# Gate and up of a SwiGLU block by seven products of halves instead of eight, with weight sums made once and fp32 transposes

## The chip, the cores and the metric

One core of one Trainium2 chip runs the whole kernel in one launch. The metric is the device time of one execution in microseconds, as the median of 3 runs. TensorE (PE) multiplies, VectorE (DVE), ScalarE (ACT) and GpSimd (POOL) do elementwise work, and SyncE (SP) issues nearly all DMAs, in order, to one queue that is served by 16 DMA engines.

## The reference

One layer of a hybrid encoder over 2048 tokens of width 1024, in float32. What the change touches is its last part:

```python
h = h + rms_norm(mix, ln_mix_post)          # mix = concat of 4 mixers @ w_out
a = rms_norm(h, ln_ffn_pre)
ff = (jax.nn.silu(a @ w_ffn_gate) * (a @ w_ffn_up)) @ w_ffn_down   # D_FF = 2816
h = h + rms_norm(ff, ln_ffn_post)
```

Ahead of it stand `a @ w_in` (1024 to 3084 columns) and four causal mixers (S5, HGRN2, FoX attention, mLSTM).

## The kernel before, in words

**Number format.** Every large product is made in three matmuls: an operand x is split in hi (x rounded to fp32r, by ACT) and lo (x - hi), and hi*hi + lo*hi + hi*lo are summed in PSUM. So each 128x128 weight tile is met by three matmuls per 512 tokens.

**Stages.** Tokens come in 4 blocks of 512, in two halves of two blocks. `in_proj` (its matmuls are L279 and L297) runs over 11 chunks of columns of `w_in` for the first half, then again for the second half. At chosen chunks it calls hooks: the mixers of block 0, their set-up, and in the second half `first`, which does `pre(0)` and `proj(0)` of the block 0. Work of mixers gets a high priority, and the framework's scheduler lays the instructions of all stages into one fixed order per engine. After `in_proj`, blocks 0 to 3 are gone through: `proj(b)` (matmuls L1394), the mixers of block b+1, then the feed-forward `run(b)` (gate and up L1477, down L1502). Mixer matmuls of block b+1 are so laid between the feed-forward matmuls of block b; block 3 has none beside it.

**Transposes.** Tokens lie on partitions and must be turned to put the contraction there. `transpose_parts` (L97 to L114) splits a tile of 128 tokens in hi and lo first (L104 ACT, L105 DVE or POOL), transposes both with fp32r matmuls against an identity (L109, 16 for a tile) and copies both out of PSUM (L112 ACT, L114 DVE). It is used for 16 tiles each in `in_proj`, `pre` and `proj`.

**proj.** `proj(b)` multiplies the mixers' outputs by `w_out` in two halves of 512 columns: the first for all 4 token tiles, the second tile by tile. After a tile's second half come a chain of small steps: scale and sum of squares, the residual `b_xt` by DMA (L1427; the pool `x` has 2 buffers), DVE L1428, ACT square L1340, POOL L69 and L70, DVE L1433, then the transposes.

**Feed-forward.** For each of 22 tiles f of 128 columns, gate and up take 24 matmuls of 512 tokens each. The first two f are cut in two halves of 256 tokens, so that the first half can run before the last two token tiles are transposed. `down` takes two f at a time, 48 matmuls of 512 columns. In block 0 each weight is loaded raw into a ring of 2 tiles `wr`, split (L89 ACT, L90 POOL), and both parts are also stored to DRAM; blocks 1 to 3 load the two parts, 1 MB for each gate or up tile, into a ring of 4 `wh` and 4 `wl`.

## Time and profile before

| | |
|---|---|
| median of 3 runs | 2833.97 us (2827.44 to 2839.25) |
| the profiled execution | 2835.35 us, span 2833.6 us, mean granted clock 0.984 |
| PE busy | 2720.2 us, 96% of the span |
| PE weight loads busy | 2294.8 us, 81% |
| DVE, POOL, ACT busy | 56%, 31%, 29% |
| DMA | 605 MB, mean 214 GB/s |
| matmuls of gate and up | 4608, 30% of the chain that ended last |
| matmuls of down | 2112, 15% of that chain |

Busy time of PE counts pipelined matmuls with modelled ends, so how fast they follow each other is read from distances of their starts. A stage's share of the DMA engines tells how much room a further transfer has there.

### The profile page before, as it was taken

To read this page: it belongs to the slowest core of one execution; us is meant where nothing else is said; L and a number is where in the kernel's file an instruction comes from. 1 tells how busy PE (TensorE), PEld (TensorE's weight loads), DVE (VectorE), ACT (ScalarE), POOL (GpSimd) and SP (SyncE) were. 2 spreads that over 40 slices of the span, in tenths; PEclk is the share of its full clock that TensorE was granted. 3 is DMA by queue.
4 is the path that set the end of the run, shared out by engine and by line. 5 is a ranking of instruction groups with operands and counts; after the bars stand their busy time and mean duration, and the time that the engine had idled before them with its cause. 6 is when DMAs were issued, how large, how long until landed. Compare 5 with 4: busy or idle time off the path is not lost.

```text
span 2833.6 us, 40116 instructions
## 1 busy us (share of the span) xinstructions
PE 2720.2 (96%) x14678; PEld 2294.8 (81%) x14678; DVE 1598.5 (56%) x2587; ACT 830.7 (29%) x1596; POOL 883.9 (31%) x959
## 2 busy tenths in 40 slices
PE   6898999999999999999999999999999999999998
PEld 5797987989888788788787777888877788888886
DVE  7968456575315666875566656645665654422323
ACT  6323326333324233324221222224122332300001
POOL 7554311253215466743211235222022432100001
PEclk9999999999999999999999999999999999999999
DMA  6673595554769887686846566475655656765553
GB/s 201 207 255 135 179 289 171 169 176 154 254 191 313 279 270 252 242 295 230 288 164 210 192 207 212 153 264 210 214 184 188 196 170 230 273 211 193 190 192 139
DMA packets 323108, 605.11 MB, mean 214 GB/s; under 512 B 56160, under 2 KB 146144, under 8 KB 322656
## 3 DMA queue, kind: packets, MB, share of 16 engines
...
q0 software_dynamic: 1024, 0.07, 0.0%
...
## 4 chain that ended last, share of the span: by engine, by line
PE 72%; DVE 11%; DMA 9%; issue 3%; POOL 2%; SPq 2%; ACT 2%; DVEq 0%; POOLq 0%; ACTq 0%
PE pf L1477 30%; PE pf L1502 15%; PE pf L297 6%; PE pf L279 5%; PE pf L1394 3%; PE ps L912 2%; DMA g_h<-h_d 1%; DVE hQ L520 1%; DMA b_xt<-in_x_dram 1%; PE ps L896 1%; PE ps L895 1%; PE ps L837 1%; DVE hA L534 1%; PE pt L109 1%; DVE xl L105 1%
## 5 line engine op out<-in xcount | busy, mean ns | idle before, releaser
L1477 PE MATMUL pf<-b_ah,wl 128*128 128x512 f32 (+1 forms) x1536 | 580.0, 378 | 0.0
L1477 PE MATMUL pf<-b_ah,wh 128*128 128x512 f32 (+1 forms) x1536 | 579.6, 378 | 0.3 <-DMA wh<-wg2h 0.3
L1477 PE MATMUL pf<-b_al,wh 128*128 128x512 f32 (+1 forms) x1536 | 579.7, 379 | 0.0
L1502 PE MATMUL pf<-dh,g_h 128*128 128x512 f32 x1408 | 458.8, 395 | 1.9 <-DVE b_acc L1507 1.8
L1477 PEld LDWEIGHTS pf<-b_ah,wh 128*128 128x128 f32 x1536 | 290.4, 189 | 55.0 <-issue 0.4
L1477 PEld LDWEIGHTS pf<-b_ah,wl 128*128 128x128 f32 x1536 | 290.5, 189 | 54.8
L1477 PEld LDWEIGHTS pf<-b_al,wh 128*128 128x128 f32 x1536 | 289.6, 189 | 54.3
L1502 PEld LDWEIGHTS pf<-dh,g_h 128*128 128x128 f32 x1408 | 263.3, 188 | 57.5 <-DVE b_acc L1507 2.9
L1502 PE MATMUL pf<-dl,g_h 128*128 128x512 f32 x704 | 276.5, 393 | 0.0
L1507 DVE TENSOR_TENSOR b_acc<-b_acc,pf 128x512 f32<-128x512 f32 x320 | 215.6, 683 | 102.1 <-PE pf L1502 100.2
L909 POOL TENSOR_TENSOR f_accs<-f_accs,f_pe 128x512 f32<-128x512 f32 (+3 forms) x144 | 172.4, 1197 | 285.0 <-ACT f_pe L903 281.8
L90 POOL TENSOR_TENSOR wl<-wr,wh 128x1024 fp32r<-128x1024 f32 (+2 forms) x76 | 187.5, 2471 | 223.6 <-ACT wh L89 194.9
L905 DVE TENSOR_TENSOR f_pl<-f_pe,f_ph 128x512 fp32r<-128x512 f32 (+3 forms) x160 | 187.0, 1176 | 94.5 <-ACT f_ph L904 78.2
L297 PE MATMUL pf<-wh,aTh 128*128 128x256 f32 (+2 forms) x768 | 219.8, 287 | 2.6 <-ACT stg L323 1.6
L297 PE MATMUL pf<-wl,aTh 128*128 128x256 f32 (+2 forms) x768 | 221.4, 288 | 0.0
L297 PE MATMUL pf<-wh,aTl 128*128 128x256 f32 (+2 forms) x768 | 220.3, 287 | 0.0
L1482 DVE SCALAR_TENSOR_TENSOR g_th<-g_th,pf 128x512 f32<-128x512 f32 x88 | 60.3, 685 | 198.7 <-ACT g_th L1481 198.1
L1481 ACT ACTIVATE g_th<-pf 128x512 f32<-128x512 f32 x88 | 52.7, 599 | 399.1 <-PE pf L1477 399.0
L279 PE MATMUL pf<-aTh,wh 128*128 128x512 f32 (+1 forms) x400 | 159.8, 400 | 1.0 <-ACT hnz L304 1.0
L279 PE MATMUL pf<-aTl,wh 128*128 128x512 f32 (+1 forms) x400 | 158.3, 398 | 2.5 <-DVE aTl L114 2.5
L903 ACT ACTIVATE f_pe<-ps 128x512 f32<-128x512 f32 (+3 forms) x160 | 85.4, 534 | 252.7 <-PE ps L896 106.7
L279 PE MATMUL pf<-aTh,wl 128*128 128x512 f32 (+1 forms) x400 | 159.1, 398 | 0.0
...
## 6 DMA issues: line engine op xcount, KB each, us to landing
...
```

The lines of the kernel that those rows point to most:

```text
L90: nc.gpsimd.tensor_tensor(lo, r, f32(hi), ALU.subtract)
L279: nc.tensor.matmul(l3(pt)[:, cut], lhsT=x[k][:, s], rhs=a[:, cut, k], start=(n == 0), stop=(n == 23))
L297: nc.tensor.matmul(pt[:, :w], lhsT=a[:, t, k], rhs=x[k], start=(n == 0), stop=(n == 23))
L903: nc.scalar.activation(pe[:, cs], pt[:, cs], AF.Exp)
L905: nc.vector.tensor_tensor(pl[:, cs], pe[:, cs], f32(ph[:, cs]), ALU.subtract)
L909: nc.gpsimd.tensor_tensor(accs[:, cs], accs[:, cs], pe[:, cs], ALU.add)
L912: nc.tensor.matmul(o, lhsT=w, rhs=r[:, cs], start=(kt + n == 0), stop=(kt + n == NK))
L1394: nc.tensor.matmul(pt, lhsT=a[:, t, k], rhs=w, start=(first and i == 0), stop=(last and i == 2))
L1477: nc.tensor.matmul(l3(pt)[:, s], lhsT=x[:, k], rhs=a[:, s, k], start=(k == 0 and i == 0), stop=(k == KD - 1 and i == 2))
L1482: nc.vector.scalar_tensor_tensor(th, th, 1.0, pts[0], ALU.add, ALU.mult)
L1502: nc.tensor.matmul(pt, lhsT=a[:, s], rhs=w[:, 0], start=(m == 0), stop=(m == 3 * len(fs) - 1))
L1507: nc.vector.tensor_tensor(acc[:, t, ns], acc[:, t, ns], pt, ALU.add)
```

## The change

**Seven products.** For a pair q of f tiles, the weights form a 2x2 of blocks (two f tiles by two halves of the 1024 contraction rows), and the tokens another (halves of the rows by even and odd token tiles). Instead of 8 block products the Strassen-Winograd scheme makes 7, from 3 plain blocks and 4 sums on the weight side and 3 plain blocks and 4 sums on the token side. `product(i)` does gate and up in one PSUM tile: 2 x 4 x 3 = 24 matmuls of 256 columns. The outputs are added up from PSUM by DVE (7 adds and one ACT copy for a pair q) before the gating.

**Weight sums.** `FfnWeights.make` runs 22 times, from hooks of `in_proj` (8 in the first half, 14 in the second): it loads two raw tiles, makes 4 sums on POOL (128x512 each) and stores 7 blocks to DRAM. The same hooks copy `w_ffn_down` and `w_out` to DRAM scratch `wd_d` and `wo_d` (30 copies of 512 KB). In the feed-forward, `load(q, i)` takes the raw product weights into the `wl` tile itself and splits them there by ACT and POOL; only for i = 0, 2 and 5 are the parts kept in DRAM, so blocks 1 to 3 split 4 of 7 products again. The ring `wr` is gone there.

**Token operands.** `proj` no longer transposes each tile: for each pair of token tiles, `operands` makes four differences (DVE and POOL) and transposes 7 blocks of 512 rows. All products read a tile `U` of 14 slots, which also holds the transposed mixer outputs before.

**Transposes** take the fp32 tile itself (L111 in the new file: 8 for a tile), and the split comes at the copy out of PSUM.

**Order.** `proj(0)` moves out of `in_proj` to the front of block 0. Mixers that run beside the feed-forward get fewer buffers (for example hQ 2 for 4, f_KB 2 for 3).

```diff
-def split_load(c, pool, raw, tag, width, shape, src, key=None, part=None):
+def split_load(c, pool, tag, width, n, src, key=None, raw=None):
...
+    x = f32(lo) if raw is None else raw.tile([P, WRING], F32, name="wr")[:, 0:n]
+    src(x)
+    nc.scalar.activation(hi, x, AF.Copy)
+    nc.gpsimd.tensor_tensor(lo, x, f32(hi), ALU.subtract)
...
-    for h in range(0, KD, 4):
-        hs = slice(h * P, (h + 4) * P)
-        hi, lo = (c.phl.tile([P, 512], F32R, name=n, tag="hl") for n in ("xh", "xl"))
-        nc.scalar.activation(hi, x[:, hs], AF.Copy)
-        eng.tensor_tensor(lo, x[:, hs], f32(hi), ALU.subtract)
-        for src, dst in ((hi, dh), (lo, dl)):
-            pt = pool.tile([P, 512], F32R, name="pt", tag=tag)
-            for j in range(4):
-                nc.tensor.transpose(pt[:, j * P:(j + 1) * P], src[:, j * P:(j + 1) * P], c.identr)
-            pv = pt.rearrange("p (k t) -> p k t", k=4)
-            if src is hi:
-                nc.scalar.activation(dst[:, h:h + 4], pv, AF.Copy)
-            else:
-                nc.vector.tensor_copy(dst[:, h:h + 4], pv)
+    for h in range(0, x.shape[1] // P, 4):
+        pt = pool.tile([P, 512], F32, name="pt", tag=tag)
+        for j in range(4):
+            nc.tensor.transpose(pt[:, j * P:(j + 1) * P], x[:, (h + j) * P:(h + j + 1) * P], c.ident)
+        pv = pt.rearrange("p (k t) -> p k t", k=4)
+        nc.scalar.activation(dh[:, h:h + 4], pv, AF.Copy)
+        nc.vector.tensor_tensor(dl[:, h:h + 4], pv, f32(dh[:, h:h + 4]), ALU.subtract)
...
-        nk = 4
+        nk, nq = (4, 4) if c.side == "right" else (3, 2)
...
-        hQ = [p1.tile([P, 2, 256], F32, name=f"hQ{p}") for p in range(nk)]
+        hQ = [p1.tile([P, 2, 256], F32, name=f"hQ{p}") for p in range(nq)]
...
+    def make(self, pool, q, m):
+        nc = self.c.nc
+        r1, r2 = (pool.tile([P, D], F32, name=n, tag=n) for n in ("ws_1", "ws_2"))
+        for r, f in ((r1, 2 * q), (r2, 2 * q + 1)):
+            nc.sync.dma_start(r.rearrange("p (k n) -> p k n", k=KD), self.w[m][:, :, f * P:(f + 1) * P])
+        a, b = slice(0, 512), slice(512, D)
+        X11, X12, X21, X22 = r1[:, a], r1[:, b], r2[:, a], r2[:, b]
+        for i, s in ((0, X11), (2, X12), (5, X22)):
+            nc.sync.dma_start(self.raw[q][i][:, m * 512:m * 512 + 512], s)
+        for i, s, x, y, op in ((3, X11, X11, X21, ALU.subtract), (4, X21, X21, X22, ALU.add),
+                               (1, X22, X22, X11, ALU.subtract), (6, X12, X12, X22, ALU.subtract)):
+            nc.gpsimd.tensor_tensor(s, x, y, op)
+            nc.sync.dma_start(self.raw[q][i][:, m * 512:m * 512 + 512], s)
+
+    def load(self, q, i):
+
+        c = self.c
+        return split_load(c, c.pw, "w", WRING, D, lambda t: c.nc.sync.dma_start(t, self.raw[q][i]),
+                          f"w{q}_{i}" if i in (0, 2, 5) else None)
...
+    def y(self, t):
+
+        i = 2 * (2 * (t % 2)) + t // 2
+        return [self.U[:, j].rearrange("p (k t) -> p k t", k=KD) for j in (i, i + 2)]
+
+    def operand(self, i, j):
+
+        u = self.U[:, 2 * i + j].rearrange("p (d k t) -> p d k t", d=2, k=4)
+        return u[:, 0], u[:, 1]
...
-            transpose_parts(c, c.psS, "s", xt, ah[:, t], al[:, t], nc.vector)
+            xs.append(xt)
+            if t % 2:
+                self.operands(t // 2, *xs[-2:])
+
+    def operands(self, j, x, x1):
+
+        c, nc = self.c, self.c.nc
+        a, b = slice(0, 512), slice(512, D)
+        s1, s2 = self.row_tile(), self.row_tile()
+        T1, T2, T3, T4 = s1[:, a], s1[:, b], s2[:, a], s2[:, b]
+        nc.vector.tensor_tensor(T1, x1[:, a], x[:, a], ALU.subtract)
+        nc.vector.tensor_tensor(T2, x1[:, b], T1, ALU.subtract)
+        nc.gpsimd.tensor_tensor(T3, x1[:, b], x1[:, a], ALU.subtract)
+        nc.vector.tensor_tensor(T4, x[:, b], T2, ALU.subtract)
+        for i, v in enumerate((x[:, a], T2, x[:, b], T3, T1, T4, x1[:, b])):
+            transpose_parts(c, c.psS, "s", v, *self.operand(i, j))
...
-            for s in cuts:
-                for f, ws, pts in job:
-                    for pt, (wh, wl) in zip(pts, ws):
-                        for k in range(KD):
-                            for i, (x, a) in enumerate(((wh, ah), (wl, ah), (wh, al))):
-                                nc.tensor.matmul(l3(pt)[:, s], lhsT=x[:, k], rhs=a[:, s, k],
-                                                 start=(k == 0 and i == 0), stop=(k == KD - 1 and i == 2))
...
+            def product(i):
+                wh, wl = c.ffw.load(q, i)
+                pt = ptile()
+                pv = pt.rearrange("p (m j t) -> p m j t", m=2, j=2)
+                for m in range(2):
+                    for k in range(4):
+                        for n, (w, d) in enumerate(((wh, 0), (wl, 0), (wh, 1))):
+                            k0 = (4 * m + k) * P
+                            nc.tensor.matmul(pv[:, m], lhsT=w[:, k0:k0 + P],
+                                             rhs=attn.U[:, 2 * i:2 * i + 2, d * 512 + k * P:d * 512 + (k + 1) * P],
+                                             start=(k == n == 0), stop=(k == 3 and n == 2))
+                return pt.rearrange("p (m t) -> p m t", m=2)
...
+            nc.scalar.activation(c1[:, 0], product(0), AF.Copy)
+            add(c1[:, 1], product(1), c1[:, 0])
+            add(c1[:, 0], product(2), c1[:, 0])
+            add(c2[:, 0], product(3), c1[:, 1])
+            pt = product(4)
+            add(c1[:, 1], pt, c1[:, 1])
+            add(c2[:, 1], pt, c2[:, 0])
+            add(c1[:, 1], product(6), c1[:, 1])
+            gated(2 * q, c1)
+            add(c2[:, 0], product(5), c2[:, 0])
+            gated(2 * q + 1, c2)
...
-        gate_up((0, 1), (slice(0, 2), slice(2, 4)))
-        for f in range(2, NF):
-            gate_up((f,), (slice(0, 4),))
-            if len(pend) == 3 and f < NF - 1:
-                down(pend[:2], pend[0][0] == 0)
+        for q in range(NF // 2):
+            gate_up(q)
+            if q:
+                down(pend[:2], q == 1)
...
+        def sums(n):
+            def f():
+                for _ in range(min(n, len(units))):
+                    q, m = units.pop(0)
+                    c.ffw.make(pool, q, m)
+                    f = 2 * q + m
+                    nc.sync.dma_start(c.wd_d[f * P:(f + 1) * P], c.w_ffn_down[0, f * P:(f + 1) * P])
+                    if f < KD:
+                        nc.sync.dma_start(c.wo_d[f * P:(f + 1) * P], c.w_out[0, f * P:(f + 1) * P])
+            return f
+
+        def hooks(start, stop, n, d):
+            return {i: ([sums(n)] if start <= i < stop else []) + d.get(i, []) for i in range(11)}
...
+            sums(len(units))()
+            stack.close()
             attn = Attn(c, ctx)
-            rows = [row, lambda: attn.xtile("b_g0")]
-            attn.row = lambda: rows.pop()()
             attn.pre(0)
-            attn.proj(0)
...
-             {0: [lambda: lower_bound(c, const)], 2: [begin, hi(lambda c, b: s5_setup(c), 0)],
-              4: [hi(hgrn_mix, 0)], 8: [hi(mlstm_mix, 0)]})
+             hooks(3, 11, 1, {0: [lambda: lower_bound(c, const)], 2: [begin, hi(lambda c, b: s5_setup(c), 0)],
+                          4: [hi(hgrn_mix, 0)], 8: [hi(mlstm_mix, 0)]}))
...
-            proj(h, lambda: nullcontext(c.px), {4: [hi(hgrn_mix, 1)], 8: [first]})
+            proj(h, lambda: nullcontext(c.px), hooks(0, 7, 2, {4: [hi(hgrn_mix, 1)], 8: [first]}))
...
-            if b:
-                attn.proj(b)
+            attn.proj(b)
```

Three places in the order of the instructions. First PE in block 3, where `proj` ends and the feed-forward begins (L1394 and L1442 are the matmuls of `proj` before and now, L109 and L111 the transposes, L1477 and L1537 gate and up). Before:

```order
L1394 MATMUL pf<-dl,b_ah 128x512
L109 MATMUL pt<-identr,xh 128x128 x4
L109 MATMUL pt<-identr,xl 128x128 x4
L109 MATMUL pt<-identr,xh 128x128 x4
L109 MATMUL pt<-identr,xl 128x128 x4
L1477 MATMUL pf<-b_ah,wh 128x256
L1477 MATMUL pf<-b_ah,wl 128x256
L1477 MATMUL pf<-b_ah,wh 128x256
L1477 MATMUL pf<-b_ah,wl 128x256
L1477 MATMUL pf<-b_ah,wh 128x256
L1477 MATMUL pf<-b_ah,wl 128x256
L109 MATMUL pt<-identr,xh 128x128 x4
```

and now:

```order
L1442 MATMUL pf<-dh,b_U 128x512 x2
L1442 MATMUL pf<-dl,b_U 128x512
L111 MATMUL pt<-ident,g_h 128x128 x4
L111 MATMUL pt<-ident,b_xt 128x128 x4
L111 MATMUL pt<-ident,g_h 128x128 x12
L111 MATMUL pt<-ident,b_xt 128x128 x8
L1537 MATMUL pf<-b_U,wh 128x256
L1537 MATMUL pf<-b_U,wl 128x256
L1537 MATMUL pf<-b_U,wh 128x256 x2
L1537 MATMUL pf<-b_U,wl 128x256
```

Before, matmuls of the first cut stood between the transposes of the last token tiles. Now all 28 transposes of the first pair of tiles, and the first four of the third tile, stand ahead of the first product, and no other matmul between them.

Second, the DMA queue of SP at the same place (b_xt is the residual of a token tile, wd the down weights, ws and w weights of products). Before, the last two residuals:

```order
L1427 DMA b_xt<-in_x_dram 128x1024
L85 DMA wh<-wg1h 128x1024
L85 DMA wl<-wg1l 128x1024
L85 DMA wh<-wu1h 128x1024
L85 DMA wl<-wu1l 128x1024
L1429 DMA h_d_228<-b_acc 128x1024
L85 DMA dh<-wd_0h 128x512
L85 DMA dl<-wd_0l 128x512
L85 DMA dh<-wd_0h 128x512
L85 DMA dl<-wd_0l 128x512
L1427 DMA b_xt<-in_x_dram 128x1024
```

and now:

```order
L81 DMA dh<-wd_0h 128x512
L81 DMA dl<-wd_0l 128x512
L1625 DMA g_h1s<-h_d_301 128x1024
L81 DMA dh<-wd_0h 128x512
L81 DMA dl<-wd_0l 128x512
L81 DMA dh<-wd_1h 128x512
L81 DMA dl<-wd_1l 128x512
L81 DMA dh<-wd_1h 128x512
L1475 DMA b_xt<-in_x_dram 128x1024
L81 DMA dl<-wd_1l 128x512
L1475 DMA b_xt<-in_x_dram 128x1024
```

The residuals of the last two token tiles now both stand behind the down weights.

Third, SP's queue at the start of `in_proj` (wr is a raw tile of `w_in` that a chunk needs, wi its stored parts, ws the stores of weight blocks). Before:

```order
L94 DMA wi_0l<-wl 128x1024
L88 DMA wr<-in_w_in_dram 128x4x256
L94 DMA wi_1l<-wl 128x1024
L88 DMA wr<-in_w_in_dram 128x4x256
L241 DMA xt<-in_x_dram 128x1024 x2
L94 DMA wi_0h<-wh 128x1024
L94 DMA wi_1h<-wh 128x1024
L94 DMA wi_0l<-wl 128x1024
L88 DMA wr<-in_w_in_dram 128x4x256
```

and now the end of the same stretch:

```order
L1724 DMA wd_d<-in_w_ffn_down_dram 16x8192
L1726 DMA wo_d<-in_w_out_dram 16x8192
L241 DMA xt<-in_x_dram 128x1024 x2
L1724 DMA wd_d<-in_w_ffn_down_dram 16x8192
L90 DMA wi_0h<-wh 128x1024
L1724 DMA wd_d<-in_w_ffn_down_dram 16x8192 x4
L90 DMA wi_0l<-wl 128x1024
L100 DMA wr<-in_w_in_dram 128x4x256
L1724 DMA wd_d<-in_w_ffn_down_dram 16x8192 x7
```

The 30 copies to DRAM scratch stand nearly all (28) among the first 64 issues: 21 of them ahead of the third chunk's first raw tile.

## Rows read from the trace of the kernel before

**Rows 1.** The page, busy time of engines over the span.

```profile
PE 2720.2 (96%) x14678; PEld 2294.8 (81%) x14678; DVE 1598.5 (56%) x2587; ACT 830.7 (29%) x1596; POOL 883.9 (31%) x959
```

**Rows 2.** Windows: stretch, length, busy PE, PEld, DVE, ACT, POOL; clock, DMA share, GB/s.

```profile
0.00:370.00 370.00, 321.85 (x2085) 289.75 (x2086) 263.41 (x532) 142.54 (x260) 191.00 (x257) 0.95 0.60 199
370.00:700.00 330.00, 311.52 (x2105) 280.49 (x2105) 204.81 (x385) 125.70 (x261) 90.10 (x119) 0.98 0.57 186
840.00:1370.00 530.00, 510.46 (x2615) 423.38 (x2614) 345.18 (x493) 188.29 (x340) 285.88 (x226) 0.98 0.82 272
1370.00:1880.00 510.00, 498.00 (x2528) 409.51 (x2527) 296.43 (x468) 133.93 (x271) 131.61 (x153) 0.99 0.60 199
2478.00:2800.00 322.00, 322.00 (x1397) 262.51 (x1398) 94.62 (x139) 24.07 (x39) 0.00 (x0) 1.00 0.56 189
```

**Rows 3.** Chain of waits: start, length, what, matmuls in it.

```profile
669.76 22.84 PE pf L297 x192
...
2500.23 22.30 PE pf L1477 x96
2522.53 10.90 PE pf L1502 x48
```

**Rows 4.** Timeline of PE in block 3, first and last of 34 rows.

```profile
2460.53 0.28 PE L1477 MATMUL pf<-b_al,wh 128*128 128x256 f32 x1
...
2464.28 0.28 PE L1477 MATMUL pf<-b_al,wh 128*128 128x256 f32 x1
```

**Rows 5.** Timelines of PE around transposes, fp32 ones first, then fp32r (first of three rows).

```profile
371.45 0.66 PE L1249 MATMUL ps<-ident,s_ur 128*128 128x128 f32 x4 [0.74 <-ACT s_ur L1246]
371.87 0.37 PE L297 MATMUL pf<-wh,aTh 128*128 128x260 f32 x1
...
2456.34 0.46 PE L109 MATMUL pt<-identr,xl 128*128 128x128 f32 x4
...
2457.32 0.35 PE L1477 MATMUL pf<-b_al,wh 128*128 128x256 f32 x1
```

**Rows 6.** Chain of waits at the end of `proj` in block 3.

```profile
2443.00 3.69 DMA b_xt<-in_x_dram
...
2451.41 7.69 DMA b_xt<-in_x_dram
...
2459.23 1.29 DVE b_acc L1428
...
2462.70 1.30 DVE b_xt L1433
...
2464.02 0.64 ACT xh L104
```

**Rows 7.** Windows around `proj` of blocks 1 and 3, columns as in rows 2.

```profile
1370.00:1425.00 55.00, 47.55 (x296) 41.10 (x295) 28.89 (x36) 19.18 (x40) 8.94 (x20) 0.94 0.64 227
...
2400.00:2478.00 78.00, 76.89 (x476) 66.88 (x475) 42.17 (x50) 24.99 (x50) 14.79 (x25) 1.00 0.77 268
```

**Rows 8.** Groups by form: busy us, mean ns of one, idle before and its releasers.

```profile
L90 POOL TENSOR_TENSOR wl<-wr,wh 128x1024 fp32r<-128x1024 f32 x72 | 176.9, 2461 | 220.0 <-ACT wh L89 191.2 <-DMA hk<-hk_d 8.3 <-PE ps L912 6.1
L89 ACT ACTIVATE wh<-wr 128x1024 fp32r<-128x1024 f32 x72 | 76.0, 1056 | 67.4 <-DMA wr<-in_w_ffn_gate_dram 21.0 <-PE pf L1477 15.0 <-DMA wr<-in_w_ffn_up_dram 7.8
L114 DVE CAST b_al<-pt 128x512 fp32r<-128x512 f32 x64 | 43.1, 687 | 46.1 <-PE pt L109 45.8
L112 ACT ACTIVATE b_ah<-pt 128x512 fp32r<-128x512 f32 x64 | 38.0, 598 | 60.8 <-PE pt L109 50.9 <-PE pf L1477 9.3
L1477 PEld LDWEIGHTS pf<-b_ah,wh 128*128 128x128 f32 x1536 | 290.4, 189 | 55.0 <-issue 0.4
```

**Rows 9.** Chain of waits: the weight loads that it ran through.

```profile
1242.61 10.65 DMA wr<-in_w_ffn_gate_dram
...
2472.17 5.70 DMA wh<-wg2h
```

165 lines of the change are left out of this document (88 added, 77 removed).

## The prediction

> **What bounds the kernel now.** I read the busy times of the page first. PE is busy for 96% of the span [rows 1], so time is gained by taking work from PE and lost by making it wait. The windows come next [rows 2]: in block 3 (the last of the rows) PE is busy without a gap and the 16 DMA engines are at 0.56; beside block 0 (840 to 1370 us) they are at 0.82. A share of 0.82 goes with 272 GB/s and 0.56 with 189, so the engines saturate near 334 GB/s. Then the chain of waits, for the pace of matmuls [rows 3]: 96 of 512 columns in 22.30 us, 0.2323 us each, and the 48 matmuls of one `down` in 10.90 us. For the new form the timeline of the first cut of gate and up serves [rows 4]: 34 starts of 256-column matmuls within 3.75 us, so 0.1136 us each.
>
> **The change part by part.** The base is the profiled execution of 2835.35 us; the median of the runs lies 1.4 us below it.
>
> *Gate and up.* Before, a block has 192 matmuls of 256 columns and 960 of 512, in four blocks 768 x 0.1136 + 3840 x 0.2323 = 979.3 us. Now 4 x 11 x 168 = 7392 matmuls of 256 columns take 7392 x 0.1136 = 839.7 us: **-139.6**. The pace of other 256- to 264-column matmuls is 22.84 / 192 = 0.119 [rows 3]; with it both sides become 983.4 and 879.6, and the gain 104. I take 0.1136, since that row has the same tile form and the same operand layout, two slices of 128 from neighbouring slots. The 7 adds and the copy of a pair (0.69 us each, as DVE's reads of PSUM in [rows 8]) lie beside 20 us of matmuls and cost nothing; if DVE fell behind, four PSUM tiles would fill and PE would wait.
>
> A weight load lasts 189 ns [rows 8], longer than 0.1136 us, yet the matmuls keep that pace: the loads run under them. The Trainium skill, TensorE: Matmul & The Clock Gate, Part 3 (Packing small matmuls), says that a weight load overlaps a running matmul only when it targets other row groups, and here every load fills the array. By that rule a matmul would take 0.1136 + 0.189 = 0.303 us, and 7392 of them 2240 us, against 1850 for the old mix: 390 us more instead of 140 less. The pace in rows 4 contradicts it.
>
> *Transposes.* 768 fp32r transposes at 0.98 / 12 = 0.082 us (three rows of four) become 480 fp32 ones at 0.42 / 4 = 0.105 [rows 5]: 62.7 to 50.4 us, **-12**. The separate splits of ACT, DVE and POOL go away, off the path except at the start of `in_proj`.
>
> *The end of `proj`.* Call T the end of its last matmul. In PE's new order 28 transposes (2.9 us) follow, then four that need the third token tile's residual, then the first product; no cut of gate and up stands between any more. The third residual needs the x buffer of the first tile, which is free only after these transposes, and it stands on SP behind the down weights, which wait for buffers that the last matmuls of `proj` read. So about 3.7 MB of weights and a 0.5 MB store are issued from T-4 on; at 334 GB/s these and the residual need 14 us, and it lands near T+10. That agrees with the fourth residual of block 3 before, which took 7.69 us behind such loads, while the one ahead took 3.69 [rows 6]. From landing to the transposes the old chain took 4.9 us (2459.1 to 2464.0) [rows 6]; transposes, ACT and DVE copies add 0.4 + 0.6 + 0.7 [rows 8]. First product at T+16.6, PE idle for 13.7 us. The second product needs the fourth tile, 1.5 us later, and two sums: T+19.5, just behind the first product's 2.7 us. At block 1 an idle 7.5 us went with a granted clock of 0.94 over 55 us [rows 7], between the levels of 1.2 and 2.4 GHz, so part of the restart ran at the lower one; I add 2 us. That is 16 us for each of four blocks, less some 4 that the old order lost in the same places [rows 7]: **+60**. Bounds: residual as fast as 3.69 us, issued at T+1.5, leaves 9 idle, +25 in all; 25 us each gives +100.
>
> *`proj(0)`* moves behind `in_proj` with the same matmuls. Beside `in_proj` PE was the bound too (311.5 of 330 us in [rows 2]), so the move alone costs nothing, and its wait is in the term above.
>
> *Beside `in_proj`.* Each of 22 calls moves 2 x 0.524 + 7 x 0.262 = 2.9 MB, and 30 copies 15.7 MB: 79 MB, 237 us of all engines. The two stretches had 0.40 x 370 + 0.43 x 330 = 290 us of room [rows 2]. It fits, barely; but 21 copies, 11 MB or 33 us, stand ahead of the third chunk's raw tile, and stores that wait for POOL's sums hold up SP, with weight loads queued behind. POOL gets 88 sums of half of 2461 ns [rows 8], 108 us in 700 us, beside 281 us of its own. Lower bound -10 (the shorter way through the transposes at the start); upper: if the share can't exceed the 0.82 of block 0, room is 164 us and 73 are missing, +73. I take **+22**, a third of that, since a chunk's weights are fetched two chunks ahead.
>
> *Weights of products.* A product lasts 24 x 0.1136 = 2.73 us. The ring has four pairs, so a load that starts when a product ends must be ready three products later, after 8.2 us. A raw load must come in, then 1.06 us on ACT and 2.46 on POOL [rows 8]. With 3.69 us [rows 6] that makes 7.2 and fits; with 5.70 [rows 9] it is 1.0 late; with 10.65, as in block 0 [rows 9], 6 late. The first four products of a pair are fetched under `down` (10.9 us); the fifth and sixth, both raw, are exposed, in each of 44 pairs. POOL's splits of this form rise from 44 to 33 + 4 x 44 = 209, 108 us in each later block, where it had 380 us free [rows 2]. DMA needs 7.3 MB for a pair's 30 us, 245 GB/s, below 334; in block 0 about 163 MB in 554 us, 294 GB/s, a share of 0.88. I take 2 us a pair in block 0, 0.5 in blocks 1 and 2, where mixers' matmuls widen the window, and 0.4 in block 3: 22 + 11 + 5 = **+38**, with bounds 0 and 4 us a pair, 176. The smaller buffers of the mixers I leave at nothing: PE has gate and up between their matmuls; if that cover fails, POOL and DVE chains of hQ and f_KB show as PE waits.
>
> Sum: 2835.35 - 139.6 - 12.3 + 60 + 22 + 38 = 2803.5, and 2802 for the median.
>
> **The rivals.** *Supply becomes the bound (slower).* The chain load, ACT, POOL of the fifth and sixth product sets the pace of a pair, because it is in order behind mixers' work on POOL and ACT. Place: each pair's gate and up; price: 3 us a pair is 132 instead of 38, 2896 us. It decides once the pairs lose 84 us in all, 1.9 us each: then the time is past 2848. For it: 10.65 in [rows 9] and POOL's 0.54 beside block 0 before [rows 2]; against it: 334 GB/s are not reached after block 0.
>
> *The queue beside `in_proj`* takes its upper bound, 73 for 22: 2853 us. For it: two stretches at 0.9 and more; against it: two chunks of lead.
>
> *Everything hides.* The residuals land early (+25 for 60), `in_proj` and the weights cost nothing: 2802 - 35 - 22 - 38 = 2707 us. For it: block 3 before lost only 1.1 us at the same place [rows 7]; against it: the order of SP and the 8.2 us.
>
> *Weight loads become the pace* of the short matmuls, 0.189 us each [rows 8]: 7392 x 0.189 = 1397, 557 more than summed, 3359 us. Against it stands the pace in [rows 4]. It is the mechanism of the skill's rule above in its mildest form.
>
> That the change does not do what it says can be left out: the new order holds 7392 matmuls of products and 480 transposes.
>
> **How the numbers follow.** Chances: forecast 0.54, supply 0.22, everything hides 0.12, `in_proj` queue 0.10, weight loads 0.02. A measurement of this kernel can tell about 0.5% from no change, 14 us: 2820 and 2848. My forecast's own range, from the bounds of its terms, is 2762 to 2842; 0.42 of its 0.54 lie below 2820, 0.09 within, 0.03 above. The rival without costs adds 0.12 to faster; supply gives 0.20 to slower and 0.02 to same, the queue 0.07 and 0.03, the loads 0.02. So faster 0.54, same 0.14, slower 0.32. For 8 in 10 the range reaches from 2735, between forecast and full gain, to 2900, just past the supply case.
>
> **What would show it.** Products start 0.114 us apart, and block 3's eleven pairs last about 30.4 us each. Between the last matmul of `proj` and the first product PE is idle for about 14 us in each block, released through the residual's DMA. PE waits in products for POOL's split of `wl` sum to about 38 us. `in_proj` up to the start of `proj(0)` ends near 810 us (840, where [rows 2] begin block 0, - 44.6 for the 192 matmuls of `proj(0)` - 7 of transposes + 22). The forecast is wrong if products start more than 0.12 us apart, if POOL's splits release PE for over 100 us, or if the idle after `proj` is below 8 or above 25 us a block.

## The result, and the profile after

The changed kernel takes 2920.8 us (median; 2912.3 to 2926.5) against 2833.0 for the kernel before: a ratio of 1.0307, with a 95% interval of 1.0269 to 1.0345. It is slower by 88 us, where 32 less were forecast, and lies outside the range of 2735 to 2900. The profiled execution took 2926.05 us, with a span of 2924.3 and a mean granted clock of 0.961 (before 0.984).

The page's busy times, which answer to [rows 1]:

```profile
PE 2650.6 (91%) x17174; PEld 2370.3 (81%) x17174; DVE 1963.9 (67%) x2879; ACT 980.5 (34%) x1737; POOL 1398.3 (48%) x1184
```

PE has 70 us less to do and is idle for 160 us more. DVE has 365 us more, POOL 514. To see in which stage the time went I took from both timelines of PE the first matmul of each `proj` and of each feed-forward, and so the length of every stretch (us; "first product" is the first gate and up matmul of block 0, and in the kernel before that stretch holds `proj(0)`, too; experiments further down stand in the same table):

| run | to first product | FF 0 | proj 1 | FF 1 | proj 2 | FF 2 | proj 3 | FF 3 to end |
|---|---|---|---|---|---|---|---|---|
| before | 839.7 | 509.5 | 57.3 | 479.0 | 48.0 | 469.3 | 48.6 | 382.2 |
| after | 894.4 | 547.6 | 64.2 | 472.6 | 63.7 | 458.3 | 62.7 | 360.9 |
| e1, no POOL split | 890.8 | 479.3 | 69.7 | 451.7 | 62.6 | 446.7 | 62.0 | 350.3 |
| e9, memset for it | 887.3 | 481.9 | 66.8 | 449.0 | 62.5 | 446.2 | 62.7 | 350.5 |
| e10, split on DVE | 890.5 | 518.8 | 80.1 | 463.0 | 60.5 | 450.7 | 61.5 | 351.6 |
| e5, all parts kept | 890.1 | 562.8 | 66.4 | 451.8 | 61.7 | 444.2 | 61.1 | 351.1 |
| e6, early residual | 893.6 | 542.8 | 59.4 | 475.2 | 60.7 | 460.9 | 60.0 | 358.5 |
| e11, e5 + e6 + e10 | 881.9 | 551.7 | 70.9 | 454.0 | 52.7 | 445.1 | 52.7 | 350.2 |
| e12, before + fp32 transposes | 826.4 | 507.6 | 58.2 | 473.1 | 47.6 | 467.5 | 47.6 | 382.2 |
| e13, no weight sums | 877.1 | 542.5 | 67.2 | 469.1 | 62.0 | 459.9 | 64.5 | 358.1 |

The four feed-forward stages took 1840.0 us before and take 1839.4 now. That is where the forecast went wrong: it had them 102 us shorter (139.6 of gate and up, less 38 for weights). The three later `proj` take 36.7 us more and the stretch up to the first product 54.7 more; -0.6 + 36.7 + 54.7 = 90.8 is the difference of the spans, within rounding. Of the 119 us by which the forecast of 2802 missed, 101 lie in the feed-forward.

The windows of the first and the last feed-forward stage, which answer to the last rows of [rows 2] (stretch, length, busy PE, PEld, DVE, ACT, POOL; clock, DMA share, GB/s):

```profile
894.41:1442.00 547.59, 483.67 (x3220) 437.29 (x3221) 436.72 (x570) 217.74 (x369) 337.11 (x233) 0.95 0.73 248
...
2563.38:2912.00 348.62, 341.72 (x2395) 314.10 (x2396) 191.64 (x243) 82.30 (x112) 108.43 (x50) 0.99 0.67 222
```

In block 0 DVE is at 80% and the DMA engines only at 0.73 (0.82 before), so no queue of transfers fills that stage. PE's five longest waits in the whole span, summed by what ended them (us in total, times, the longest):

```profile
PE pt L111 <- DVE b_xt L1481: 36.7, 4, 11.0
PE ps L530 <- DVE hQ L520: 27.4, 16, 5.9
PE ps L914 <- DVE f_pl L907: 24.6, 24, 6.6
PE pt L111 <- DVE xt L248: 20.5, 7, 9.9
PE pt L111 <- DVE g_h L1493: 18.7, 7, 11.4
```

All five end with DVE (the first of them comes after the late residual at the end of `proj`, further down). In the four feed-forward stages PE's waits sum to 106 us, 80 of them ended by DVE; before they were 27 and 20. POOL's split `wl` released the products for 1.7 us in all, and ACT's rounding `wh` for 5.4, where 38 were forecast for the chain of both. The matmuls follow each other more slowly than forecast, too: with these waits taken out, gate and up take 901 us of PE, 0.122 us a matmul, not 0.1136.

What DVE does in these waits is seen in its groups by form, in the kernel before:

```profile
L905 DVE TENSOR_TENSOR f_pl<-f_pe,f_ph 128x512 fp32r<-128x512 f32 x112 | 152.9, 1372 | 72.1 <-ACT f_ph L904 63.8 <-PE ps L912 5.9 <-issue 1.4
L1487 DVE SCALAR_TENSOR_TENSOR g_h<-g_th,g_h 128x512 fp32r<-128x512 f32 x88 | 84.5, 960 | 34.0 <-ACT g_h L1486 33.4
...
L1482 DVE SCALAR_TENSOR_TENSOR g_th<-g_th,pf 128x512 f32<-128x512 f32 x88 | 60.3, 685 | 198.7 <-ACT g_th L1481 198.1
```

and in the changed one:

```profile
L1543 DVE TENSOR_TENSOR g_c<-pf,g_c 128x512 f32<-128x512 f32 x308 | 206.9, 684 | 199.7 <-PE pf L1537 198.8
L907 DVE TENSOR_TENSOR f_pl<-f_pe,f_ph 128x512 fp32r<-128x512 f32 x112 | 155.1, 1392 | 44.1 <-ACT f_ph L906 41.7 <-PE ps L914 2.0
L1549 DVE SCALAR_TENSOR_TENSOR g_th<-g_th,g_c 128x512 f32<-128x512 f32 x88 | 127.1, 1444 | 61.5 <-ACT g_th L1548 60.8
...
L86 POOL TENSOR_TENSOR wl<-wl,wh 128x1024 fp32r<-128x1024 f32 x215 | 525.3, 2446 | 639.0 <-ACT wh L85 588.6 <-PE pf L1537 26.6 <-DMA dl<-wd_0l 10.2
```

Each of these groups of DVE's has 512 columns. Those with an input in PSUM (`pf`) take 0.685 us in both kernels. Those with two inputs in SBUF take from 0.96 to 1.44 on the mean, as far as shown here; the first step of the gating went from the one kind to the other, since its operand is now the SBUF tile `g_c`. How an instruction of 0.68 us gets so long the timelines tell. In the usual case it is one split that stands in the way, as here at a step of the gating (DVE's row, then POOL's two):

```profile
1657.70 2.89 DVE L1549 SCALAR_TENSOR_TENSOR g_th<-g_th,g_c 128x512 f32<-128x512 f32 x1
1657.67 2.38 POOL L86 TENSOR_TENSOR wl<-wl,wh 128x1024 fp32r<-128x1024 f32 x1 [2.24 <-ACT wh L85]
1660.00 1.72 POOL L911 TENSOR_TENSOR f_accs<-f_accs,f_pe 128x512 f32<-128x512 f32 x1
```

The step ends at 1660.59, 0.54 us after the split, and POOL's next instruction goes on beyond it. The longest case, in block 0, is another:

```profile
1063.93 1.26 DVE L1585 TENSOR_TENSOR b_acc<-b_acc,pf 128x512 f32<-128x512 f32 x2
1065.12 9.51 DVE L907 TENSOR_TENSOR f_pl<-f_pe,f_ph 128x512 fp32r<-128x512 f32 x1
```

and POOL's at the same time:

```profile
1065.02 2.42 POOL L86 TENSOR_TENSOR wl<-wl,wh 128x1024 fp32r<-128x1024 f32 x1
1067.37 0.62 POOL L909 COPY f_accs<-f_pe 128x512 f32<-128x512 f32 x1
1067.94 3.70 POOL L86 TENSOR_TENSOR dl<-dl,dh 128x512 fp32r<-128x512 f32 x3
1071.61 1.25 POOL L911 TENSOR_TENSOR f_accs<-f_accs,f_pe 128x512 f32<-128x512 f32 x1
1072.83 1.25 POOL L86 TENSOR_TENSOR dl<-dl,dh 128x512 fp32r<-128x512 f32 x1
```

POOL works without a gap from 1065.02 to 1074.08, and `f_pl` ends at 1074.63. DVE's instructions over 2 us were 41 with 107 us in all before, and are 118 with 305 us now. Of the 118, 55 ended, as in the usual case, while POOL went straight on to its next instruction; four of `f_pl` in block 0 were passed by two to six further instructions of POOL, 26 us in all.

The Trainium skill, SBUF — State Buffer (SBUF: two separate sides), says that DVE and GpSimd share one pair of SBUF ports as an exclusive lock, which a DVE instruction needs in a two-port mode or with two SBUF inputs, the latter only against a GpSimd instruction that reads SBUF. The Trainium skill has the lock held for one instruction there. The 55 agree with it; the four of `f_pl` do not, and for them the measurement decides.

So the theory to test was: **POOL's 209 splits of product weights (44 of this form were there before) shut out DVE; DVE's in-order queue falls behind; PE waits for DVE.** Its rivals: DVE's own new work (seven adds a pair); the chain load, ACT, POOL as a chain (the supply rival of the prediction); the mixers' smaller buffers; and POOL's own queue, in which steps of the mixers stand behind splits.

### The profile page after: what moved, and what is told of

Same layout as the page of the kernel before. It is cut to its first block, busy times and chain, and to the rows that moved or that the text cites. A ratio compares the mean times of both kernels' runs of the same rounds, so it can differ in the third digit from the quotient of the medians.

```text
span 2924.3 us, 46692 instructions
## 1 busy us (share of the span) xinstructions
PE 2650.6 (91%) x17174; PEld 2370.3 (81%) x17174; DVE 1963.9 (67%) x2879; ACT 980.5 (34%) x1737; POOL 1398.3 (48%) x1184
## 3 DMA queue, kind: packets, MB, share of 16 engines
q0 software_dynamic: 1024, 0.07, 0.0%
## 4 chain that ended last, share of the span: by engine, by line
PE 45%; DVE 23%; DMA 15%; POOL 5%; issue 5%; ACT 4%; SPq 2%; DVEq 0%; POOLq 0%; ACTq 0%
PE pf L1537 19%; PE pf L1580 6%; DMA wl<-ws 5%; PE pf L297 4%; PE pf L279 3%; PE pf L1442 3%; DVE g_th L1549 3%; DVE f_pl L907 2%; DVE hQ L520 2%; DVE b_acc L1585 2%; PE ps L914 1%; DVE g_th L1550 1%; PE pt L111 1%; DMA ws<-ws 1%; POOL wl L86 1%
## 5 line engine op out<-in xcount | busy, mean ns | idle before, releaser
L1537 PE MATMUL pf<-b_U,wh 128*128 128x256 f32 x4928 | 923.6, 284 | 9.7 <-ACT wh L85 5.4
L86 POOL TENSOR_TENSOR wl<-wl,wh 128x1024 fp32r<-128x1024 f32 x215 | 525.3, 2446 | 639.0 <-ACT wh L85 588.6
L1537 PEld LDWEIGHTS pf<-b_U,wh 128*128 128x128 f32 x4928 | 780.5, 192 | 23.6 <-ACT wh L85 6.3
L1537 PE MATMUL pf<-b_U,wl 128*128 128x256 f32 x2464 | 698.7, 284 | 2.1 <-POOL wl L86 1.7
L1537 PEld LDWEIGHTS pf<-b_U,wl 128*128 128x128 f32 x2464 | 472.3, 192 | 9.3 <-POOL wl L86 4.1
L85 ACT ACTIVATE wh<-wl 128x1024 fp32r<-128x1024 f32 x215 | 227.4, 1058 | 427.2 <-DMA wl<-ws 366.6
L1543 DVE TENSOR_TENSOR g_c<-pf,g_c 128x512 f32<-128x512 f32 x308 | 206.9, 684 | 199.7 <-PE pf L1537 198.8
L1549 DVE SCALAR_TENSOR_TENSOR g_th<-g_th,g_c 128x512 f32<-128x512 f32 x88 | 127.1, 1444 | 61.5 <-ACT g_th L1548 60.8
L297 PEld LDWEIGHTS pf<-wh,aTh 128*128 128x128 f32 x768 | 150.2, 196 | 13.7 <-ACT stg L323 9.2
L1369 POOL TENSOR_TENSOR ws<-ws,ws 128x512 f32<-128x512 f32 x66 | 92.1, 1396 | 131.8 <-DMA ws<-ws 104.0
```

The costliest lines, as they stand in the source:

```text
L85: nc.scalar.activation(hi, x, AF.Copy)
L86: nc.gpsimd.tensor_tensor(lo, x, f32(hi), ALU.subtract)
L297: nc.tensor.matmul(pt[:, :w], lhsT=a[:, t, k], rhs=x[k], start=(n == 0), stop=(n == 23))
L1369: nc.gpsimd.tensor_tensor(s, x, y, op)
L1537: nc.tensor.matmul(pv[:, m], lhsT=w[:, k0:k0 + P], rhs=attn.U[:, 2 * i:2 * i + 2, d * 512 + k * P:d * 512 + (k + 1) * P], start=(k == n == ...
L1543: nc.vector.tensor_tensor(dst, pt, x, ALU.add)
```

## Experiments

**e1: POOL's subtraction left out for the weights of products.**

```diff
-    nc.gpsimd.tensor_tensor(lo, x, f32(hi), ALU.subtract)
+    if sub:
+        nc.gpsimd.tensor_tensor(lo, x, f32(hi), ALU.subtract)
```

(`sub` is false in `FfnWeights.load` alone.)

> Edit: POOL's subtraction for the weights of the products (215 of 2.45 us, 525 us) is left out, so the lo part of these weights stays the raw weight; loads, ACT's rounding, the adds and all matmuls stay. The changed kernel's feed-forward stages take as long in all as before (0.8 us less), where 140 us less were summed. Theory 1 (POOL's splits hold up DVE's instructions that read two SBUF tiles, and DVE's lateness makes PE wait): the gating's first step falls from a mean of 1.44 to about 0.7 us, no instruction of DVE lasts over 3 us, and the time falls by 60 to 90 us, to 2830 to 2860. Theory 2 (DVE is late because of its own new work, seven adds a pair): POOL matters little, the time falls by less than 20 us, over 2900. Theory 3 (the chain load, ACT, POOL paces the products): 2.45 us of the chain are gone, so the time falls too, 40 to 80 us, 2840 to 2880; only the next run separates it from theory 1.

Measured: 2812.5 us, ratio to before 0.9923 (0.9898 to 0.9948); 108 us less than the changed kernel, more than the 60 to 90 that theory 1 gave. (The edit takes out 209 splits, 511 us; the six of `proj`'s weights stay.) DVE's groups by form:

```profile
L908 DVE TENSOR_TENSOR f_pl<-f_pe,f_ph 128x512 fp32r<-128x512 f32 x112 | 124.7, 1117 | 69.6 <-ACT f_ph L907 68.0 <-PE ps L915 1.1
...
L1550 DVE SCALAR_TENSOR_TENSOR g_th<-g_th,g_c 128x512 f32<-128x512 f32 x88 | 64.2, 729 | 78.0 <-ACT g_th L1549 77.2
```

The gating's first step takes 0.729 us for 1.444, and 20 instructions of DVE are over 2 us instead of 118. The feed-forward stages take 1728.0 us, 111 less than in the changed kernel, 68 of them in block 0. There the window shows what went with it:

```profile
890.80:1370.10 479.30, 456.72 (x3221) 417.28 (x3222) 336.51 (x573) 216.58 (x369) 158.66 (x160) 1.00 0.81 283
```

DVE is busy for 100 us less with the same instructions, and the granted clock is 1.00 for 0.95. Over the four stages PE's waits that end with DVE fall from 80 to 11 us; all others stay at 26. So 68 of the 111 us are waits for DVE, and in the other 43 PE's matmuls follow each other faster.

**e2: the same subtraction, written where no product reads it.**

```diff
-    nc.gpsimd.tensor_tensor(lo, x, f32(hi), ALU.subtract)
+    nc.gpsimd.tensor_tensor(lo if aside is None else aside, x, f32(hi), ALU.subtract)
```

(`aside`, a scratch tile, is given for the weights of products alone.)

> Edit: POOL makes the same subtraction of the same operands at the same place, but writes it to a scratch tile that no product reads (bf16, for room), so the lo part of the product weights stays the raw weight. No product waits for POOL. Theory 1 (POOL's activity holds up DVE): as slow as the changed kernel, 2905 to 2925, with DVE's gating step still near 1.4 us. Theory 2 (adds): the same time, too, since nothing that it names has changed. Theory 3 (the supply chain): as fast as without the split, within 15 us of the run without the subtraction.

Measured: 2946.7 us, ratio 1.0397 (1.0372 to 1.0423). No product waits for POOL, and nothing is won: POOL's link in the supply chain falls as the cause, and the other two, load and ACT, stand in e1 as well. That it is even 26 us slower than the changed kernel was not expected. The 26 us lie in the feed-forward stages (1866.0 us), where PE's waits for DVE are 96 us for 80, and DVE has 135 instructions over 2 us, 343 us in all: more of the same. Why there are more of them stays open; that ACT's squares share the scratch tile isn't enough of a reason, since they share it in e9 further down, too, and nothing is lost there.

**e3 and e4: the seven adds left out, with POOL's splits and without.**

```diff
-            add(c1[:, 1], product(1), c1[:, 0])
-            add(c1[:, 0], product(2), c1[:, 0])
-            add(c2[:, 0], product(3), c1[:, 1])
+            product(1)
+            product(2)
+            product(3)
...
-            add(c1[:, 1], product(6), c1[:, 1])
+            nc.scalar.activation(c1[:, 1], product(6), AF.Copy)
```

> Edit: the seven adds of a pair on DVE are left out; products 4, 5 and 6 are copied by ACT (as product 0 is), products 1 to 3 are not read. So the sums of the seven products are left out of the output. POOL's splits and the gating from SBUF stay. DVE loses 308 x 0.684 = 211 us. Theory 1 (POOL holds up DVE): the long instructions of DVE stay (gating near 1.4 us), DVE has a little more room, the time falls by 15 to 35 us, 2885 to 2905. Theory 2 (DVE's own work): the time falls by 60 to 90 us, 2830 to 2860. Theory 3 (supply): within 10 us of 2921.

> Edit: both of the last: neither the adds on DVE nor POOL's subtraction for product weights. If DVE's lateness, by POOL or by its own work, is all that the feed-forward lost, its four stages come within 20 us of the 140 us that the matmuls save: 2921 - 120 = about 2800. If theory 1 alone holds, this is within 15 us of the run without the subtraction; if theory 2 alone holds, within 15 us of the run without the adds. If both stay above 2860, something else in the feed-forward (mixers' smaller buffers, the queue of DMAs) takes the gain.

(In both ACT copies three of the products instead; the second part of the cut shows one.) Measured: 2910.4 us for e3, ratio 1.0281 (1.0249 to 1.0314), and 2800.2 for e4, ratio 0.9888 (0.9865 to 0.9911). So 211 us less of DVE's own work give 10 to 12 us; e3 lies 5 us above theory 1's range. Without POOL's splits the four feed-forward stages take 1727.1 us with no adds and 1728.0 with them: the adds as such cost nothing there. DVE's own work isn't the cause.

**e9: a memset in place of the subtraction.** What e1 and e2 can't separate is the port from POOL's queue.

```diff
-    nc.gpsimd.tensor_tensor(lo, x, f32(hi), ALU.subtract)
+    if aside is None:
+        nc.gpsimd.tensor_tensor(lo, x, f32(hi), ALU.subtract)
+    else:
+        nc.gpsimd.tensor_tensor(aside.bitcast(F32)[:, 0:1], x[:, 0:1], f32(hi)[:, 0:1], ALU.subtract)
+        nc.gpsimd.memset(aside.bitcast(U8), 0)
```

> Edit: in place of the subtraction for product weights POOL makes a difference of one column and a memset of a scratch tile (2048 bytes a partition), so it is about as long in the same places of its queue, waits for the same weights, but hardly reads SBUF. The lo part of the product weights stays the raw weight. It tells apart two ways in which POOL's splits could hold up the rest. Port (a subtraction that reads SBUF shuts out DVE's instructions with two SBUF inputs): these run at their own pace (f_pl 512 columns near 1.1 us, gating near 0.73), and the time is within 25 us of the run without the subtraction, 2812 to 2837. Queue (mixers' own steps on POOL stand in order behind the splits, and PE waits for what follows from them): DVE's instructions are short, too, but the time stays above 2880.

Measured: 2810.4 us, ratio 0.9916 (0.9891 to 0.9940), as without the subtraction (e1). Groups by form, POOL's memset, one of DVE's, and POOL's one-column difference:

```profile
L90 POOL MEMSET junk<- 128x2048 uint8 x209 | 377.3, 1805 | 10.9
...
L911 DVE TENSOR_TENSOR f_pl<-f_pe,f_ph 128x512 fp32r<-128x512 f32 x112 | 122.3, 1097 | 59.2 <-ACT f_ph L910 55.2 <-PE ps L918 3.7 <-DMA wd_0h<-dh 0.2
...
L89 POOL TENSOR_TENSOR junk<-wl,wh 128x1 f32<-128x1 f32 x209 | 52.3, 250 | 565.2 <-ACT wh L85 559.0 <-ACT lsa L178 3.1 <-POOL mvw L732 0.5
```

In each of these places POOL now works for 2.05 us (1.805 + 0.250) where the split took 2.45; its share of the span is 46% for 48, and mixers' steps still stand in one queue with it. Yet the whole 108 us come back. POOL's queue is not the cause. In e2 POOL reads both tiles and writes the same scratch tile of 2048 bytes a partition, and the time is as long as ever; here it hardly reads and writes that tile, and the time comes back. So what counts is that POOL reads SBUF. The sentence of the Trainium skill above makes that the condition.

**e7: gating reads PSUM.** The last sum is written back to its PSUM tile, and each half is gated from there.

```diff
...
-            add(c1[:, 1], product(6), c1[:, 1])
-            gated(2 * q, c1)
...
+            pt = product(6)
+            add(pt, pt, c1[:, 1])
+            gated(h[0], 1, pt)
...
```

> Edit: the last sum of each gated half is written back to its PSUM tile and the gating reads it there, half by half (12 instructions of 256 columns for a pair where there were 6 of 512). DVE has as much to do; its first two gating steps no longer read two SBUF tiles. POOL's splits stay. Theory 1 (POOL holds up only those of DVE's instructions that read two SBUF tiles): these steps run at their own pace, about 0.35 us for 256 columns; DVE gets back some 90 us of its 1964, the waits of down for DVE (about 25 us) nearly go; the time falls by 20 to 50 us, 2870 to 2900; f_pl and hQ stay long. Rival (DVE is slow for POOL whatever it reads, or PSUM tiles are held too long): within 10 us of 2921 or slower.

Measured: 2922.7 us, ratio 1.0305 (1.0278 to 1.0331): no gain, as the rival had it, but not by the rival's reason. DVE's groups by form:

```profile
L1552 DVE SCALAR_TENSOR_TENSOR g_h<-g_th,g_h 128x256 fp32r<-128x256 f32 x176 | 178.8, 1016 | 29.0 <-ACT g_h L1551 28.6
...
L1549 DVE SCALAR_TENSOR_TENSOR g_th<-g_th,pf 128x256 f32<-128x256 f32 x176 | 73.2, 416 | 95.6 <-ACT g_th L1548 95.1
```

The first two steps of the gating, 214.6 us in the changed kernel, take 146.6; the last one, which still has two SBUF inputs, went from 80.8 to 178.8. The shut-out moved to the next instruction that can be shut out. So this run can't say what the gating alone costs.

**e8: the mixers' smaller buffers, alone, on the kernel before.**

```diff
-        hQ = [p1.tile([P, 2, 256], F32, name=f"hQ{p}") for p in range(nk)]
+        hQ = [p1.tile([P, 2, 256], F32, name=f"hQ{p}") for p in range(nq)]
...
-("f_KB", min(b + 2, 3), (1.0, 1.0))
+("f_KB", min(b + 2, 3 if c.side == "right" else 2), (1.0, 1.0))
```

> Edit, on the kernel before: the mixers beside the feed-forward get the buffers that they have in the changed kernel (hQ 2 for 4, hK 3 for 4, f_KB 2 for 3, p 4 for 5, two tiles of S5 single, msg and mvw in pieces), and nothing else. The prediction's term: nothing, within 10 us of the kernel before. Rival (the smaller buffers are part of what the feed-forward lost: without POOL's splits its four stages still lack 28 us of the 140): 15 to 30 us slower than before, with PE's waits for hQ and f_KB up by as much.

Measured: 2839.8 us, ratio 1.0026 (1.0015 to 1.0038). Seven microseconds: real, but small.

**e5: the parts of all seven products kept**, so that blocks 1 to 3 split none.

```diff
-                          f"w{q}_{i}" if i in (0, 2, 5) else None)
+                          f"w{q}_{i}")
```

> Edit: block 0 stores the two parts of all seven products' weights (before: of three), so blocks 1 to 3 load them and POOL splits none there: 132 of 209 splits go, and 132 of ACT's roundings. A later pair then loads 7 MB for 5, and block 0 stores 44 MB more. Theory (POOL's splits hold up DVE): feed-forward stages 1 to 3 gain what the run without the subtraction gained there, 21 + 12 + 11 = 44 us; block 0 keeps its POOL and gets 80 GB/s on top of 248, close to saturation, which costs it 0 to 40. So 2877 to 2917 us. Rival (DMA is what matters): blocks 1 to 3 lose as well, with a DMA share over 0.85 there, and the time is above 2921.

Measured: 2892.5 us, ratio 1.0210 (1.0188 to 1.0231). The table has the theory's 45 us in blocks 1 to 3 (20.8 + 14.1 + 9.8), and 15 us lost in block 0, whose splits stay and which now stores 44 MB more.

**e10: the splits on DVE.**

```diff
-    nc.gpsimd.tensor_tensor(lo, x, f32(hi), ALU.subtract)
+    (nc.gpsimd if eng is None else eng).tensor_tensor(lo, x, f32(hi), ALU.subtract)
```

(`eng` is DVE for the weights of products alone.)

> Edit: the subtraction for product weights is done by DVE instead of POOL; all is computed. A 1024-column instruction of DVE takes 1.29 us (b_xt), so DVE gets 215 x 1.29 = 277 us more, on 1754 without POOL's hold-ups: 2030, 70% of the span. Port theory: cheaper than POOL's 525 us of shut-out, 2830 to 2860. If DVE's queue is what counts, whoever fills it, the splits now stand in front of its mixer and gating steps: over 2890.

Measured: 2878.8 us, ratio 1.0152 (1.0132 to 1.0173). Faster than with POOL's splits by 42 us, though DVE is now busier (1998.4 us for 1963.9):

```profile
L86 DVE TENSOR_TENSOR wl<-wl,wh 128x1024 fp32r<-128x1024 f32 x209 | 262.0, 1254 | 150.4 <-ACT wh L85 149.2 <-DMA wl<-ws 0.8
...
L1549 DVE SCALAR_TENSOR_TENSOR g_th<-g_th,g_c 128x512 f32<-128x512 f32 x88 | 70.0, 796 | 9.0 <-ACT g_th L1548 8.4
```

It misses the port theory's range by 19 us, and is 66 us slower than e1, with no split at all: in block 0 alone it takes 40 us more than e1, so there DVE's own queue counts, too.

**e6 and e11: the end of `proj`.** In e6 the late residuals go to idle tiles; e11 is e5, e6 and e10 together.

```diff
-            xt = self.xtile("b_xt")
+            xt = self.xtile("b_xt") if t < 2 else self.late[t - 2]()
...
+    attn.late = [lambda: p1.tile([P, D], F32, name="g_c1", tag="g_c1"), lambda: p1.tile([P, D], F32, name="g_c2", tag="g_c2")]
...
```

> Edit: the residuals of the third and fourth token tile of proj go to the tiles g_c1 and g_c2, which are idle during proj, in place of the two x tiles that wait for the transposes of the first pair. No memory is added. Theory (the prediction's: the late residual makes the idle after proj, 11 us in the trace): the waits of transposes for b_xt (36.7 us in four) fall to under 12 in all, proj to the first product lasts about 53 us a block for 63, and the time falls by 25 to 45 us, to 2876 to 2896. Rival (the chain of DVE, ACT and POOL steps on the last tiles ends last anyway, so the residual's landing matters little): the time falls by less than 12 us.

> Edit: three together: the parts of all seven products kept (splits only in block 0), these splits on DVE, and the late residuals in idle tiles. All is computed. If the gains add: feed-forward of blocks 1 to 3 as with all parts kept (45 us less than in the changed kernel), block 0 near 500 us for 548, proj 9 us less: 2921 - 45 - 48 - 9 = about 2820, faster than the kernel before by some 10 us. If block 0 is bound by its DMAs (44 MB of stores more) or by DVE, it stays at 545 and the time is near 2865.

Measured: e6 2904.6 us, ratio 1.0248 (1.0227 to 1.0269), 16 us less than the changed kernel and so between theory (25 to 45) and rival (under 12); `proj` fell to 60, not to 53. A piece of the chain of waits of e6 there, in block 3:

```profile
2546.05 3.36 DVE b_acc L1476
```

This `b_acc` (1.28 us on the mean in e1) is shut out by a split that POOL does from 2545.98 to 2548.33. In e11, where POOL splits no weights of products, `proj` of blocks 2 and 3 takes the 52.7 us that were expected (block 1 takes 70.9). e11 as a whole takes 2868.6 us, ratio 1.0114 (1.0091 to 1.0137): its block 0 stays at 551.7, with PE's waits

```profile
PE pf L1538 <- ACT wh L85: 17.7, 7, 5.5
PE pf L1538 <- DVE wl L86: 15.3, 13, 1.8
```

Here, with 44 MB more to store and the splits in DVE's queue, the supply of weights is late indeed: 33 us, where the same two waits (for ACT and POOL) are 7 us in the changed kernel.

**e12: the transposes alone, on the kernel before.**

```diff
...
-            for j in range(4):
-                nc.tensor.transpose(pt[:, j * P:(j + 1) * P], src[:, j * P:(j + 1) * P], c.identr)
...
+        for j in range(4):
+            nc.tensor.transpose(pt[:, j * P:(j + 1) * P], x[:, (h + j) * P:(h + j + 1) * P], c.ident)
...
```

> Edit, on the kernel before: only the transposes of the change, fp32 tiles as they are, 384 for 768, with the split at the copy out of PSUM; all is computed. By the prediction's prices 768 x 0.082 = 63 us of PE become 384 x 0.105 = 40, so 22 us less while PE is busy with them, and the splits ahead of the first transposes leave the path at the start: 2800 to 2818 us. If the transposes were hidden or the copies out of PSUM (DVE subtracts now) make PE wait: within 8 us of before.

Measured: 2809.2 us, ratio 0.9907 (0.9888 to 0.9926). It computes all, and it beats both kernels: 26 us under the one before.

**e13 and e14: what `in_proj` pays for.** e13 leaves POOL's 88 weight sums out, e14 issues the 30 copies to DRAM scratch from ACT.

```diff
-            nc.gpsimd.tensor_tensor(s, x, y, op)
```

```diff
-                    nc.sync.dma_start(c.wd_d[f * P:(f + 1) * P], c.w_ffn_down[0, f * P:(f + 1) * P])
+                    nc.scalar.dma_start(c.wd_d[f * P:(f + 1) * P], c.w_ffn_down[0, f * P:(f + 1) * P])
...
```

> Edit: POOL's 88 sums of weight blocks beside in_proj are left out; the blocks are stored unsummed (so the output is that of other weights). All DMAs, stores and copies stay. in_proj lasts 819 us up to proj(0) in the changed kernel; with fp32 transposes alone on the kernel before it lasts about 780 without its proj(0), so the sums, stores and copies cost about 40, where 22 were forecast. Port theory: the sums (123 us of POOL that read SBUF) shut out DVE's steps with two SBUF inputs there (mcv 1.10 us for 0.86), and with them gone in_proj loses 10 to 20 us, 2900 to 2910. Queue of DMAs: nothing is gained, 2915 to 2925.

> Edit: the 30 copies of the down and output weights to DRAM scratch are issued by ACT instead of SP; all is computed. The same bytes move, but no raw tile of in_proj stands behind them in SP's order. If SP's order is the cost: in_proj up to proj(0) falls by 10 to 25 us, 2896 to 2910. If the bytes are the cost, or if the chunks' lead covers both: within 8 us of 2921.

Measured: e13 2902.6 us, ratio 1.0240 (1.0225 to 1.0256), with 17 us less up to the first product; DVE's `mcv` (L362, two SBUF inputs) takes 0.894 us there for 1.096. e14 takes 2940.9 us, ratio 1.0356 (1.0319 to 1.0392), with 20 us more up to the first product. Taking the copies out of SP's order does not help, so that order wasn't shown to cost anything. The loss of e14 is at the very start: in the first 80 us PE waits 39.0 us for the transposes' input `xt`, for 14.8 in the changed kernel, and ACT waits 15.5 us for the DMA of `xt`, for 4.8. That the copies, issued earlier, hold up these loads fits, but no run shows it. Nearly half of the 40 us that the work beside `in_proj` costs (worked out below) is POOL's sums.

## Why the prediction was wrong

**The step that failed is "weights of products".** It priced POOL's splits as latency, 38 us of waits in all, and held their busy time against the time that POOL had free. Both are about POOL and PE. Whom POOL's work shuts out was not asked. Measured, the splits cost 108 us by e1 and 110 by e9, and hardly any of it as a wait of products for POOL, which is

```profile
PE pf L1537 <- POOL wl L86: 1.7, 3, 1.3
```

The second half of the same mistake stands under "gate and up": the adds "cost nothing", which e4 confirms, but the sentence took DVE's 0.69 us for every instruction. In block 0 the loss grew by itself: PE waits for 64 us, its granted clock is 0.95, and its matmuls get longer.

The trace before had shown it. [rows 2] have DVE at 65% beside block 0 and POOL at 54%; the rows of L1487 and L1482 above have the same columns and 0.960 against 0.685 us. Not all of that is POOL: in e1 the last step of the gating still takes 0.756.

**Gate and up** (-139.6). Without POOL's splits the feed-forward is 102.4 us shorter than with the transposes alone (1728.0 against 1830.4 in e12). That is near the 104 which the pace of 0.119 in [rows 3] had given as the other end. With PE's waits taken out, gate and up take 994.6 us in e12 and 887.5 in e1, where 979.3 and 839.7 were forecast. A whole pair in block 3 of e1 lasts 30.2 us, as forecast (30.4). Of the 48 us that are missing 43 are in the blocks in which mixers' matmuls stand between the products (0.121 to 0.122 us a matmul, 0.1163 in block 3). The 0.1136 was the fastest row, and was taken for all. The changed kernel's 0.122 lies past the 0.12 that the prediction had named as a sign of being wrong; e1's 0.120 shows that the splits make little of that.

**Weight loads as the pace** (3359 us): no. In block 3 of e1 168 matmuls of products take 19.25 us, 0.1146 each, while a load lasts 0.19.

**The end of `proj`** (+60) held, size and cause. Between the last matmul of `proj` and the first product PE is idle for 17.9, 11.7, 14.3 and 13.5 us in the four blocks, forecast 13.7. In block 3:

```profile
2547.02 0.63 PE L111 MATMUL pt<-ident,g_h 128*128 128x128 f32 x4 [1.44 <-DVE g_h L1493]
...
2549.33 0.65 PE L111 MATMUL pt<-ident,g_h 128*128 128x128 f32 x4 [0.37 <-DVE b_U L114]
2549.93 0.66 PE L111 MATMUL pt<-ident,b_xt 128*128 128x128 f32 x4
2561.61 1.08 PE L111 MATMUL pt<-ident,b_xt 128*128 128x128 f32 x4 [11.03 <-DVE b_xt L1481]
2563.38 0.58 PE L1537 MATMUL pf<-b_U,wh 128*128 128x256 f32 x1 [0.69 <-ACT b_U L113]
```

(PE's timeline; the idle time ahead of each row and its releaser stand in brackets.) The chain of waits has the residual landing at 2556.25, 10.7 us after the last matmul of `proj`, where T+10 was forecast:

```profile
2549.70 6.55 DMA b_xt<-in_x_dram
...
2556.69 1.30 DVE b_acc L1476
```

This answers to [rows 6]. `proj` of blocks 1 to 3 grew by 36.7 us, 12 each. With the residual early and no splits on POOL (e11) 3.3 to 3.5 us of idle time are left there in these three blocks.

**Beside `in_proj`** (+22). `proj(0)` starts at 819.1 us where 810 were forecast. Against e12, whose transposes are the same, the stretch to the first product is 68 us longer; 28 of these are the longer `proj(0)` (75.3 against 47.6 in a later block of e12), and 40 remain for sums, stores and copies. So the term was sized at about half (its 22 was called a third of 73, which is 24), and nearly half of the 40 is again POOL (17 us, e13).

**Transposes** (-12 for 480). 384 of them alone gave -26 where the same prices make -22. Near enough.

**Mixers' smaller buffers** at nothing: 7 us (e8). Nearly right.

**The DMA engines** were taken to saturate near 334 GB/s. That was too low: the changed kernel moves 350 GB/s in its first 73 us, and e5 377 from 1011 to 1083 us. The landing of the residual, worked out with it, came out within 1 us all the same.

**The rivals.** "Supply becomes the bound" had the right side and, at 2896, nearly the time; that is luck, since its mechanism was not there: e2 takes POOL out of the products' chain and wins nothing. The sign given for it, POOL's splits releasing PE for over 100 us, isn't in the trace: 1.7 us.
